# Hybrid decoder layer on one core: all decay blocks of an HGRN2 head in one TensorE visit, ordered by tile width

## The chip, the cores and the metric

The kernel runs on one core of a Trainium2 chip. The metric is the device time of one execution in microseconds (us); lower is better. TensorE (PE in the profile) does matrix products, VectorE (DVE) and ScalarE (ACT) do element-wise work, SyncE (SP) issues the loads from HBM.

## What is computed

One layer of a decoder for 256 tokens of width 2048, in float32: a token mixer with two branches (HGRN2, a gated linear attention with 16 heads of 128 channels, and Mamba-2 with 8 groups), then a cross attention into 256 memory tokens, then a gated convolutional feed-forward part and a last norm. The change lies in the HGRN2 branch, with a small part in Mamba-2. Cut to that:

```python
def gla_chunk_scan(q, k, v, log_f):
    ...
        b = jnp.cumsum(gc, axis=1)
        o_inter = jnp.einsum('bthk,bhkv->bthv', qc * jnp.exp(b), state)
        decay = masked_decay(b[:, :, None] - b[:, None, :])
        scores = jnp.einsum('bthk,btshk,bshk->bhts', qc, decay, kc)
        o_intra = jnp.einsum('bhts,bshv->bthv', scores, vc)
    ...
def hgrn2_branch(q_raw, f_raw, i_raw, og_raw, lb, norm_g):
    ...
    o = gla_chunk_scan(q, k, v, log_f)
    o = o * jax.nn.sigmoid(og_raw...)
    o = o * lax.rsqrt(jnp.mean(o * o, axis=-1, keepdims=True) + NORM_EPS)
    o = o * norm_g
```

The kernel does not walk through the tokens. For every head it makes the whole matrix A[s, t] of decayed scores (source token s, target token t, s not after t), and then weighs the values with it.

## The kernel before, in words

**The main stream.** Nearly all work is products of 256 tokens with large weight matrices. A weight piece of 1 MB comes by DMA into `raw`; ACT casts it (line 103) into a high part `hi`, and DVE makes the rest `lo` (line 104), half a piece at a time, both into rings of five halves. `project` (line 171 on) takes one piece and makes 16 pairs of products on TensorE: `hi` with 512 columns (lines 157, 159) and `lo` with 256 columns (lines 156, 160). `project_tok` (lines 189 to 191) takes four pieces and makes token rows with 512 columns each; it is called once for every four heads. Operands of these products are float32r; the small products described below are plain float32, which the profile shows as two passes per product (two instructions).

**Side work in steps.** The recurrences are generators in the list `background`. Every call of `weights()`, that is, every time the main stream takes the next piece, calls `step()`, and every generator in the list then runs on to its next `yield`, the oldest first. So the side work's products come into TensorE's queue between two pieces: such a group of small products is called a visit here. One head of HGRN2 takes three pieces (query, forget gate, output gate; lines 376 to 384), and every fourth head four more before them (values). Only when a head's three projections are issued does its generator `hg_scan` enter the list. Its steps fall on the next six pieces:

1. Step 0 (lines 390 to 429): the gates. ACT and DVE make log f and its running sum `bb`, then differences and their exponentials for the levels of half width 2, 4, 8, 16, 32 and 64 (tiles `e0`, `e1`; view `lev`) and for the two halves of 128 tokens (`ec`).
2. Step 1 (lines 431 to 438): DVE multiplies them with keys and queries.
3. Step 2 (lines 447 to 465): TensorE makes the blocks of the levels 1 to 16: products whose left operand has 32 columns, so that four of them fill the four column groups of the array (lines 449 and 455), into the PSUM tile `lp`. DVE merges them into `sm` with masks (lines 459 to 464).
4. Step 3 (lines 467 to 487): TensorE makes, for each half of the tokens, the two blocks of level 32 (left operand of 32 columns, line 471) and the block of level 64 (64 columns, line 474), then the block between the halves (128 columns, line 477), into a `misc` tile. DVE and ACT copy everything into A (tile `a`; lines 480 to 487).
5. Step 4 (lines 490 to 496): TensorE weighs the values with A (lines 490, 491), DVE multiplies with the output gate `so` (line 492), and the squares are split in two parts (`sqs`, lines 494 to 496).
6. Step 5 (lines 498 to 506): TensorE sums the squares (line 500), ACT makes the norm, DVE applies it and splits the result (lines 504, 506).

With three pieces per head, steps 3, 4 and 5 of a head fall on the same pieces as steps 0, 1 and 2 of the next, except behind every fourth head.

**The order on each engine** is set when the program is built. A planner goes through the instructions in program order, and may put an instruction that it takes to be ready ahead of one that it takes to be waiting. On the chip every engine works through its own queue in that order and waits on semaphores.

**Mamba-2** has the same form: `m2_scan` (line 568 on) is a generator whose third visit makes the squares' sum (line 624); one group takes six pieces.

The names that matter: `pm_` ("misc", two PSUM tiles), `pl` ("lev", two PSUM tiles), `so` (two buffers), `ab` (two tiles A).

Of the kernel before, what the change touches and what calls it, by code (L numbers as in the profile page):

```python
# [9 lines left out]
F32 = mybir.dt.float32  # L10
# [9 lines left out]
P = 128  # L20
T = 256
# [6 lines left out]
HEADS = 16  # L28
GROUPS = 8
# [13 lines left out]
SMALL = 5  # L43
B = 32
# [5 lines left out]
def hybrid_trunk(ctx, tc, xT, memT, par, cst, msk, w_ka, w_va, w_hg, w_hv, w_ghg, w_bhg, w_dt,  # L50
# [13 lines left out]

# [1 line left out]
    order = [w_ka[n] for n in range(KD)]  # L66
# [26 lines left out]
    def halves(w, c, d):  # L93
        """Both float32r parts of the columns c..d of a piece of weights."""
        raw, cols, parts = w
        half = (cols // 256) * 128
        a, b = (0, half) if c < half else (half, cols)
        if c == a:
            hi = wp.tile([P, 1024], F32R, name="hi", bufs=WB)
            lo = wp.tile([P, 1024], F32R, name="lo", bufs=WB)  # L100
            parts.append((a, b, hi, lo))
        _, _, hi, lo = parts[-1]
        S.copy(out=hi[:, c - a:d - a], in_=raw[:, c:d])  # L103
        V.tensor_tensor(out=lo[:, c - a:d - a], in0=raw[:, c:d],  # L104
                        in1=hi[:, c - a:d - a].bitcast(F32), op=ALU.subtract)
# [23 lines left out]
    def drain():  # L129
        while background:  # L130
            step()

    def prefetch(ahead):
        while state["issued"] < min(state["used"] + ahead, len(order)):
            issue()
# [15 lines left out]

# [1 line left out]
    def hl_pair(ps, wh, wl, hl, first, last):  # L153
        """ps[:, 0:T] + ps[:, T:2T] gathers w @ x, but for the product of both low parts."""
        if last:
            PE.matmul(ps[:, 0:T], lhsT=wl, rhs=hl[:, 0:T], start=False, stop=False)  # L156
            PE.matmul(ps, lhsT=wh, rhs=hl, start=first, stop=True)  # L157
        else:
            PE.matmul(ps, lhsT=wh, rhs=hl, start=first, stop=False)  # L159
            PE.matmul(ps[:, 0:T], lhsT=wl, rhs=hl[:, 0:T], start=False, stop=False)  # L160
# [17 lines left out]
    def project_tok(hl):  # L178
        """Token rows: [128 tokens, 512 channels] for both halves of the tokens."""
        ps = [pj.tile([P, 512], F32, name="proj") for _ in range(2)]  # L180
        for i in range(4):
            w = weights()
            for j in range(4):
                k = 4 * i + j
                wh, wl = w(j, 512)
                for g in range(2):
                    x1 = hl[:, k, g * P:(g + 1) * P]
                    x2 = hl[:, k, T + g * P:T + (g + 1) * P]
                    PE.matmul(ps[g], lhsT=x1, rhs=wh, start=(k == 0), stop=False)  # L189
                    PE.matmul(ps[g], lhsT=x1, rhs=wl, start=False, stop=False)  # L190
                    PE.matmul(ps[g], lhsT=x2, rhs=wh, start=False, stop=(k == KD - 1))  # L191
        return ps
# [33 lines left out]
    def row_rsqrt(pool, out, acc):  # L226
        """1/rms of every token, on all partitions."""
        ps = pm_.tile([P, 512], F32, name="misc")
        PE.matmul(ps[:, 0:T], lhsT=ones, rhs=acc, start=True, stop=True)
        rsqrt(out, ps[:, 0:T], 1.0 / D, eps_t)  # L230

    def col_rsqrt(out, acc):
        """1/rms of every token, tokens on partitions."""
        ps = pm_.tile([P, 512], F32, name="misc")
        for g in range(2):
            PE.matmul(ps[:, g:g + 1], lhsT=acc[:, g * P:(g + 1) * P], rhs=ones[:, 0:1],
                      start=True, stop=True)
        rsqrt(out, ps[:, 0:2], 1.0 / D, eps_t)

# [1 line left out]
    s1 = big.tile([P, KD, 512], F32R, name="s1")  # L241
# [25 lines left out]
    with tc.tile_pool(name="st", bufs=1) as st:  # L267
# [6 lines left out]
        r_xb = st.tile([P, T], F32, name="r_xb")  # L274
        # the first chunks advance together, so that the products need little data at a time
        nc.sync.dma_start(out=par_t[:, 0:8 * KD], in_=par[:, 0:8 * KD])
# [45 lines left out]

        # lower bounds and the per-channel constants made of them
        lb = st.tile([P, 4, KD], F32, name="lb")
# [26 lines left out]

# [1 line left out]
    def softplus_neg_abs(x, w, absolute=False):  # L353
        """w = ln(1 + exp(-|x|))"""
        if not absolute:
            S.activation(out=w, in_=x, func=AF.Abs)
            x = w
        S.activation(out=w, in_=x, func=AF.Exp, scale=-1.0)
        S.activation(out=w, in_=w, func=AF.Ln, bias=1.0)
# [27 lines left out]
    def hg_scan(h, kq, zz, v):  # L387
# [17 lines left out]
        S.activation(out=kq[:, 0, :], in_=t, func=AF.Exp, scale=-1.0)  # L405
        so = mp.tile([P, T], F32, name="so", bufs=2)
        V.scalar_tensor_tensor(out=so, in0=zz[:, 1, :], scalar=0.0, in1=w[:, 1, :],
                               op0=ALU.min, op1=ALU.subtract)
        S.activation(out=so, in_=so, func=AF.Exp)

        # decayed keys (left half of a block) and queries (right half), per level; in blocks of
        # two tokens the left factor is one and the right one is the token's own decay
        ql = mp.tile([P, T // B, B + B // 2], F32, name="ql", bufs=1)
# [26 lines left out]

        # A[s, t]: own block of the first half | second half seen from the first | own block.
        # Within blocks of 32 tokens the levels are merged on a compact [s, half, t of the block].
        a = ab[h % 2]
        lp = pl.tile([P, 512], F32, name="lev")
        W1 = B + B // 2
        for g in range(2):
            for blk in range(P // B):
# [3 lines left out]
            for i, hw in enumerate(LEVELS[1:SMALL]):  # L451
                o = 2 * W1 + (2 * i + g) * B
                for blk in range(P // B):
                    t0 = g * P + blk * B
                    PE.matmul(lp[blk * B:(blk + 1) * B, o:o + B], lhsT=lev[hw][:, t0:t0 + B],  # L455
                              rhs=lev[hw][:, t0:t0 + B], start=True, stop=True)
        sm = mp.tile([P, 2, B], F32, name="sm", bufs=1)
        l0 = lp[:, 0:2 * W1].rearrange("p (g t) -> p g t", g=2)
# [3 lines left out]
        for i in range(1, SMALL):  # L462
            o = 2 * W1 + 2 * (i - 1) * B
            V.copy_predicated(out=sm, mask=free(msk_t, i * B, [(0, 2), (1, B)]),
                              data=lp[:, o:o + 2 * B].rearrange("p (g t) -> p g t", g=2))
        yield True
        ps = pm_.tile([P, 512], F32, name="misc")
        for g in range(2):
            for s0 in (0, 2 * B):
                t0 = g * P + s0  # L470
                PE.matmul(ps[s0:s0 + B, g * B:(g + 1) * B], lhsT=lev[32][:, t0:t0 + B],  # L471
                          rhs=lev[32][:, t0 + B:t0 + 2 * B], start=True, stop=True)
            t0 = g * P
            PE.matmul(ps[0:2 * B, P + 2 * g * B:P + 2 * (g + 1) * B],  # L474
                      lhsT=lev[64][:, t0:t0 + 2 * B], rhs=lev[64][:, t0 + 2 * B:t0 + 4 * B],
                      start=True, stop=True)
        PE.matmul(ps[:, T:3 * P], lhsT=ec[:, 0:P], rhs=ec[:, P:T], start=True, stop=True)  # L477
        for blk in range(P // B):
            rows = slice(blk * B, (blk + 1) * B)
            V.tensor_copy(out=free(a[rows, :], blk * B, [(2 * P, 2), (1, B)]), in_=sm[rows])  # L480
        for s0 in (0, 2 * B):
            rows = slice(s0, s0 + B)
            V.tensor_copy(out=free(a[rows, :], s0 + B, [(2 * P, 2), (1, B)]),
                          in_=ps[rows, 0:2 * B].rearrange("p (g t) -> p g t", g=2))
        V.tensor_copy(out=free(a[0:2 * B, :], 2 * B, [(2 * P, 2), (1, 2 * B)]),
                      in_=ps[0:2 * B, P:T].rearrange("p (g t) -> p g t", g=2))
        S.copy(out=a[:, P:2 * P], in_=ps[:, T:3 * P])
        yield True
        ps = pm_.tile([P, 512], F32, name="misc")
# [6 lines left out]
        split(sqs, sq)  # L496
        yield True
        ps = pm_.tile([P, 512], F32, name="misc")
# [12 lines left out]

# [1 line left out]
    dt_tok = cp.tile([P, 2, 32], F32, name="dt_tok")  # L513
    cum_tok = cp.tile([P, 2, 32], F32, name="cum_tok")

    def m2_dt():
# [14 lines left out]
        V.memset(one[0:32], 1.0)  # L531
        cum = mp.tile([P, T], F32, name="so", bufs=2)
        V.tensor_tensor_scan(out=cum[0:32], data0=one[0:32], data1=w[0:32], initial=0.0,
# [34 lines left out]
    def m2_scan(g, sz, cb):  # L568
# [50 lines left out]
        V.tensor_tensor(out=sq[:, 0, :], in0=sq[:, 0, :], in1=sq[:, 1, :], op=ALU.add)  # L619
        yield True  # L620
        if g + 1 < GROUPS:
            yield True
        ps = pm_.tile([P, 512], F32, name="misc")
# [44 lines left out]

# [1 line left out]
    xp = ctx.enter_context(ExitStack())  # L670
# [104 lines left out]

# [1 line left out]
    fp = ctx.enter_context(tc.tile_pool(name="fp", bufs=1))  # L777
# [67 lines left out]

# [1 line left out]
def _cols(w):  # L847
    """[K, N] -> [N/128, 128 rows of a k block, K/128 * 128]"""
    k, n = w.shape
# [4 lines left out]
def _toks(w):  # L854
    """[K, N] -> [N/512, 4, 128 rows of a k block, 4 * 512]"""
    k, n = w.shape
# [91 lines left out]
```

## Time and profile before

| | |
|---|---|
| device time, three runs | 2317.78 us median (2317.59 to 2318.37) |
| the profiled execution: its span | 2318.0 us (0.2 us above the median of the runs) |
| granted TensorE clock, mean | 0.998 |
| HGRN2: from the first visit to the last | 155.2 to 542.1 us of the span |
| Mamba-2: from its first visit to its last | 728.7 to 1017.0 us of the span |

The profiled execution's own time is its span, 2318.0 us. A row of the timeline has the start in us, the duration in us, the engine, the line, the operation, output<-input tiles and the number of instructions merged. A TensorE instruction's duration includes the way through the array, so starts, not durations, tell what a product costs in a stream: the next one starts before the last one has ended.

### The profile page before, as it was taken

The page shows a single profiled execution, that of the slowest core. Times are in us where ns is not written, and L with a number is a line of the kernel's source. Part 1 is how long each engine was busy: PE and PEld are TensorE (multiplying, and loading weights), DVE is VectorE, ACT ScalarE, POOL GpSimd, SP SyncE. Part 2 cuts the span into 40 slices and gives each one's busy share as a digit, 9 for nine tenths or more (in the row PEclk, how much of TensorE's full clock was granted, in tenths as well). Part 3 has the DMA queues.
Part 4 walks back from the last instruction along what each step waited for, and adds up shares of the span by engine and source line. Part 5 has one row for each costly group of instructions (what it writes and reads, how often), then busy time and mean ns, then how long its engine had stood idle before and what let it go on. Part 6 is the DMA issues. An engine that isn't in the chain of part 4 may idle for free.

```text
span 2318.0 us, 35910 instructions
## 1 busy us (share of the span) xinstructions
PE 2298.1 (99%) x14210; PEld 1983.4 (86%) x14210; DVE 1610.9 (69%) x2652; ACT 1348.4 (58%) x2126; POOL 1.3 (0%) x9
## 2 busy tenths in 40 slices
PE   8999999999999999999999999999999999999998
PEld 7888888888888888888888888888888888888887
DVE  7768879797556777765676755667777777765554
ACT  7566767676445778764455645555555555544443
POOL 0000000000000000000000000000000000000000
PEclk9999999999999999999999999999999999999999
DMA  7654444445555455445566544555555555545554
GB/s 276 243 182 162 167 164 164 164 164 208 184 183 190 174 190 184 180 173 190 182 232 213 206 167 164 186 213 187 186 190 188 182 185 191 187 159 195 197 194 141
DMA packets 74953, 433.93 MB, mean 187 GB/s; under 512 B 8321, under 2 KB 15905, under 8 KB 31009
## 3 DMA queue, kind: packets, MB, share of 16 engines
q1 hardware_dynamic: 74208, 430.72, 52.7%
q8 instruction: 112, 1.84, 0.3%
q10 hardware_dynamic: 576, 0.92, 0.1%
q14 instruction: 57, 0.46, 0.1%
HBM read 425.28 MB, written 6.32 MB: 186 GB/s over the span
## 4 chain that ended last, share of the span: by engine, by line
PE 98%; DVE 1%; ACT 0%; DMA 0%; SPq 0%; issue 0%; DVEq 0%; ACTq 0%
PE proj L159 53%; PE proj L160 27%; PE proj L157 3%; PE proj L189 3%; PE proj L191 3%; PE proj L190 3%; PE proj L156 2%; PE misc L159 0%; DMA mraw<-in_memT 0%; PE lev L455 0%; PE misc L608 0%; PE misc L474 0%; PE misc L490 0%; PE misc L477 0%; PE misc L471 0%; PE misc L157 0%
## 5 line engine op out<-in xcount | busy, mean ns | idle before, releaser
L159 PE MATMUL proj<-s,hi 128*128 128x512 f32 x4935 | 1760.9, 399 | 9.9 <-ACT hi L103 5.5
L160 PE MATMUL proj<-s,lo 128*128 128x256 f32 x4935 | 1385.1, 281 | 0.0
L104 DVE TENSOR_TENSOR lo<-raw,hi 128x1024 fp32r<-128x1024 f32 (+4 forms) x827 | 956.8, 1161 | 410.3 <-ACT hi L103 402.4
L159 PEld LDWEIGHTS proj<-s,hi 128*128 128x128 f32 x4935 | 928.3, 188 | 223.6 <-ACT hi L103 11.3
L103 ACT CAST hi<-raw 128x1024 fp32r<-128x1024 f32 (+4 forms) x827 | 824.2, 998 | 431.2 <-PE proj L159 284.1
L160 PEld LDWEIGHTS proj<-s,lo 128*128 128x128 f32 x4935 | 933.1, 189 | 12.5 <-DVE lo L104 0.3
L196 ACT COPY jt<-proj 128x256 f32<-128x256 f32 x265 | 98.4, 372 | 384.2 <-PE proj L157 384.1
L157 PE MATMUL proj<-s,hi 128*128 128x512 f32 x313 | 124.9, 399 | 0.0
L159 PE MATMUL proj<-ha,hi 128*128 128x512 f32 x300 | 106.5, 398 | 0.0
L189 PE MATMUL proj<-hi,s 128*128 128x512 f32 x256 | 101.0, 395 | 0.0
L191 PE MATMUL proj<-hi,s 128*128 128x512 f32 x256 | 99.8, 390 | 0.0
L190 PE MATMUL proj<-lo,s 128*128 128x512 f32 x256 | 99.7, 389 | 0.0
L156 PE MATMUL proj<-s,lo 128*128 128x256 f32 x313 | 88.2, 282 | 0.0
L160 PE MATMUL proj<-ha,lo 128*128 128x256 f32 x300 | 84.2, 281 | 0.0
L156 PEld LDWEIGHTS proj<-s,lo 128*128 128x128 f32 x313 | 58.8, 188 | 15.2
L159 PEld LDWEIGHTS proj<-ha,hi 128*128 128x128 f32 x300 | 56.4, 188 | 13.3
L157 PEld LDWEIGHTS proj<-s,hi 128*128 128x128 f32 x313 | 59.3, 190 | 0.2 <-DVE s L212 0.2
L197 DVE TENSOR_TENSOR t<-proj,jt 128x256 f32<-128x256 f32 x65 | 27.5, 424 | 44.6 <-ACT jt L196 44.5
L160 PEld LDWEIGHTS proj<-ha,lo 128*128 128x128 f32 x300 | 56.7, 189 | 0.7
L191 PEld LDWEIGHTS proj<-hi,s 128*128 128x128 f32 x256 | 48.0, 188 | 10.2
L190 PEld LDWEIGHTS proj<-lo,s 128*128 128x128 f32 x256 | 48.1, 188 | 9.6
L189 PEld LDWEIGHTS proj<-hi,s 128*128 128x128 f32 x256 | 48.1, 188 | 9.4
(273 smaller groups left out, 1682.7 us busy)
## 6 DMA issues: line engine op xcount, KB each, us to landing
raw<-in_w_up SPq DMA_DIRECT2D x88, 1024.0 KB, 4.8
raw<-in_w_hg SPq DMA_DIRECT2D x48, 1024.0 KB, 4.8
raw<-in_w_m SPq DMA_DIRECT2D x48, 1024.0 KB, 4.8
raw<-in_w_dn SPq DMA_DIRECT2D x64, 704.0 KB, 4.1
raw<-in_w_hv SPq DMA_DIRECT2D x16, 1024.0 KB, 4.9
raw<-in_w_ghg SPq DMA_DIRECT2D x16, 1024.0 KB, 4.8
raw<-in_w_bhg SPq DMA_DIRECT2D x16, 1024.0 KB, 4.8
raw<-in_w_gm SPq DMA_DIRECT2D x16, 1024.0 KB, 4.8
```

What stands on the lines that cost most here:

```text
L103: S.copy(out=hi[:, c - a:d - a], in_=raw[:, c:d])
L104: V.tensor_tensor(out=lo[:, c - a:d - a], in0=raw[:, c:d], in1=hi[:, c - a:d - a].bitcast(F32), op=ALU.subtract)
L156: PE.matmul(ps[:, 0:T], lhsT=wl, rhs=hl[:, 0:T], start=False, stop=False)
L157: PE.matmul(ps, lhsT=wh, rhs=hl, start=first, stop=True)
L159: PE.matmul(ps, lhsT=wh, rhs=hl, start=first, stop=False)
L160: PE.matmul(ps[:, 0:T], lhsT=wl, rhs=hl[:, 0:T], start=False, stop=False)
L189: PE.matmul(ps[g], lhsT=x1, rhs=wh, start=(k == 0), stop=False)
L190: PE.matmul(ps[g], lhsT=x1, rhs=wl, start=False, stop=False)
L191: PE.matmul(ps[g], lhsT=x2, rhs=wh, start=False, stop=(k == KD - 1))
L196: S.copy(out=tmp, in_=ps[:, T:2 * T])
L197: V.tensor_tensor(out=out, in0=ps[:, 0:T], in1=tmp, op=ALU.add)
```

## The change

Step 3's products move into step 2, ahead of the narrow ones, so that one visit makes all blocks in the order 128, 64 and 32 columns. The block between the halves gets a second `lev` tile (`ep`), the blocks of the levels 64 and 32 go into the unused columns of `lp`, and the two level-64 blocks now lie in the two column halves of the array. The weighing and the norm come three steps later each, where the next head's blocks are made: in the same visit come, in this order, the norm of head h-2, the weighing of head h-1 and the blocks of head h. The copies into A follow at once. `so` has four buffers in place of two. In Mamba-2 the norm of a group comes three steps later, with the visit of the next group's first products.

```diff
+    def pause(n):
+        for _ in range(n):
+            yield True
...
-        so = mp.tile([P, T], F32, name="so", bufs=2)
+        so = mp.tile([P, T], F32, name="ho", bufs=4)
...
         lp = pl.tile([P, 512], F32, name="lev")
+        ep = pl.tile([P, 512], F32, name="lev")
         W1 = B + B // 2
+        o32 = 2 * W1 + 2 * (SMALL - 1) * B
+        o64 = o32 + 2 * B
+        PE.matmul(ep[:, 0:P], lhsT=ec[:, 0:P], rhs=ec[:, P:T], start=True, stop=True)
+        for g in range(2):
+            t0 = g * P
+            PE.matmul(lp[g * 2 * B:(g + 1) * 2 * B, o64:o64 + 2 * B],
+                      lhsT=lev[64][:, t0:t0 + 2 * B], rhs=lev[64][:, t0 + 2 * B:t0 + 4 * B],
+                      start=True, stop=True)
+        for g in range(2):
+            for s0 in (0, 2 * B):
+                t0 = g * P + s0
+                PE.matmul(lp[s0:s0 + B, o32 + g * B:o32 + (g + 1) * B], lhsT=lev[32][:, t0:t0 + B],
+                          rhs=lev[32][:, t0 + B:t0 + 2 * B], start=True, stop=True)
         for g in range(2):
             for blk in range(P // B):
...
+        S.copy(out=a[:, P:2 * P], in_=ep[:, 0:P])
         sm = mp.tile([P, 2, B], F32, name="sm", bufs=1)
...
-        yield True
-        ps = pm_.tile([P, 512], F32, name="misc")
+        for s0 in (0, 2 * B):
+            rows = slice(s0, s0 + B)
+            V.tensor_copy(out=free(a[rows, :], s0 + B, [(2 * P, 2), (1, B)]),
+                          in_=lp[rows, o32:o64].rearrange("p (g t) -> p g t", g=2))
         for g in range(2):
-            for s0 in (0, 2 * B):
-                t0 = g * P + s0
-                PE.matmul(ps[s0:s0 + B, g * B:(g + 1) * B], lhsT=lev[32][:, t0:t0 + B],
-                          rhs=lev[32][:, t0 + B:t0 + 2 * B], start=True, stop=True)
-            t0 = g * P
-            PE.matmul(ps[0:2 * B, P + 2 * g * B:P + 2 * (g + 1) * B],
-                      lhsT=lev[64][:, t0:t0 + 2 * B], rhs=lev[64][:, t0 + 2 * B:t0 + 4 * B],
-                      start=True, stop=True)
-        PE.matmul(ps[:, T:3 * P], lhsT=ec[:, 0:P], rhs=ec[:, P:T], start=True, stop=True)
+            V.tensor_copy(out=a[0:2 * B, 2 * g * P + 2 * B:2 * g * P + 4 * B],
+                          in_=lp[g * 2 * B:(g + 1) * 2 * B, o64:o64 + 2 * B])
...
-        yield True
+        gap = 3 if h + 1 < HEADS else 2
+        yield from pause(gap)
...
-        yield True
+        yield from pause(gap)
...
-        yield True
-        if g + 1 < GROUPS:
-            yield True
+        yield from pause(5 if g + 1 < GROUPS else 1)
```

More of the change, by code (lines that the diff above doesn't have):

```diff
@@ L480, in hg_scan @@
             V.tensor_copy(out=free(a[rows, :], blk * B, [(2 * P, 2), (1, B)]), in_=sm[rows])
[L481 to L487, printed above, removed]
-        yield True
+        gap = 3 if h + 1 < HEADS else 2
+        yield from pause(gap)
         ps = pm_.tile([P, 512], F32, name="misc")
@@ L531, in m2_dt @@
         V.memset(one[0:32], 1.0)
-        cum = mp.tile([P, T], F32, name="so", bufs=2)
+        cum = mp.tile([P, T], F32, name="ho", bufs=4)
         V.tensor_tensor_scan(out=cum[0:32], data0=one[0:32], data1=w[0:32], initial=0.0,
```

## The prediction

> **What bounds the kernel now.** First the page: engine totals and the chain that ended last.
>
> ```profile
> span 2318.0 us, 35910 instructions
> PE 2298.1 (99%) x14210; PEld 1983.4 (86%) x14210; DVE 1610.9 (69%) x2652; ACT 1348.4 (58%) x2126; POOL 1.3 (0%) x9
> PE 98%; DVE 1%; ACT 0%; DMA 0%; SPq 0%; issue 0%; DVEq 0%; ACTq 0%
> ```
>
> TensorE works through its queue almost without a wait. So what counts is how far each group of instructions moves TensorE's next start; the busy column can't tell, since durations overlap. I therefore took the timeline of TensorE alone, at head 7, whose visits look like those of any head. This is step 3 (levels 32 and 64, block between the halves):
>
> ```profile
> 303.59 0.40 PE L157 MATMUL proj<-s,hi 128*128 128x512 f32 x1
> 303.92 0.26 PE L471 MATMUL misc<-e 128*32 128x32 f32 x4
> 304.11 0.33 PE L474 MATMUL misc<-e 128*64 128x64 f32 x2
> 304.37 0.26 PE L471 MATMUL misc<-e 128*32 128x32 f32 x4
> 304.55 0.33 PE L474 MATMUL misc<-e 128*64 128x64 f32 x2
> 304.81 0.49 PE L477 MATMUL misc<-ec 128*128 128x128 f32 x2
> 305.06 0.47 PE L189 MATMUL proj<-hi,s 128*128 128x512 f32 x1
> 305.37 0.39 PE L190 MATMUL proj<-lo,s 128*128 128x512 f32 x1
> 305.60 0.40 PE L191 MATMUL proj<-hi,s 128*128 128x512 f32 x1
> ```
>
> A product of 512 columns moves the next start by 0.23 us (305.37 to 305.60). So the stream could have gone on at 303.82; it goes on at 305.06, and its first product takes 0.31. The visit costs 1.24 + 0.08 = 1.32 us, for twelve small products. The tile width (128*32, 128*64, 128*128) changes five times; the entry alone, 303.82 to 303.92, is 0.10 us with nothing in it. Step 4 (weighing) and steps 5 and 2 (norm, then narrow blocks):
>
> ```profile
> 310.62 0.59 PE L490 MATMUL misc<-a,vc 128*128 128x256 f32 x2
> 311.06 0.38 PE L491 MATMUL misc<-a,vc 128*128 128x128 f32 x2
> 311.19 0.47 PE L189 MATMUL proj<-hi,s 128*128 128x512 f32 x1
> 311.51 0.39 PE L190 MATMUL proj<-lo,s 128*128 128x512 f32 x1
> ...
> 316.74 0.40 PE L500 MATMUL misc<-sqs,ones_r 128*128 128x256 f32 x2
> 317.07 0.29 PE L449 MATMUL lev<-ql,kq 128*32 128x48 f32 x8
> ...
> 317.94 0.50 PE L189 MATMUL proj<-hi,s 128*128 128x512 f32 x1
> 318.28 0.40 PE L190 MATMUL proj<-lo,s 128*128 128x512 f32 x1
> ```
>
> The weighing costs 0.57 + (0.32 - 0.23) = 0.66 us, the other visit 1.20 + (0.34 - 0.23) = 1.31. One head's side work costs 1.32 + 0.66 + 1.31 = 3.29 us of TensorE's stream, 16 heads some 53 us.
>
> DVE is the second bound. One head's period within a run of heads, in the view by stretches (stretch, length, then busy time of PE, PEld, DVE, ACT):
>
> ```profile
> 277.20:297.20 20.00, 20.00 (x197) 17.21 (x196) 18.66 (x47) 15.15 (x29) 0.00 (x0) 1.00 0.46 159
> ```
>
> 18.66 of 20.00 us: little room, and the products of step 2 need what DVE makes last.
>
> **The change part by part.**
>
> *TensorE's visits.* The joint visit has norm, weighing, block between the halves (all 128 wide), two level-64 blocks, four level-32 blocks, narrow blocks.
> - Norm: half of a 512-column product for each of two, 0.23. Weighing: 0.66, as now.
> - Block between the halves: the weighing streams 384 columns in two passes for 0.66, so 128 columns cost 0.22. Its own row is dearer (304.81 to 305.06, 0.25, and the 0.08 behind it), since it now stands behind a width change. I take 0.22; upper end 0.33.
> - Entry into the narrow widths: 0.10, as at 303.82.
> - Level 64: one block with its way out takes 0.26 (304.11 to 304.37). The two blocks now lie in two column halves. What that does, Mamba-2 shows (L584 full width, L608 in two halves):
>
> ```profile
> 728.69 0.59 PE L584 MATMUL misc<-sz 128*128 128x256 f32 x2
> 729.12 0.38 PE L585 MATMUL misc<-sz 128*128 128x128 f32 x2
> 735.43 0.66 PE L608 MATMUL misc<-e,bb 128*64 128x256 f32 x4
> 735.91 0.40 PE L610 MATMUL misc<-e,bb 128*64 128x128 f32 x4
> ```
>
>   Two passes take 0.43, four in two halves 0.48: they run side by side. So I take 0.28 for both blocks, upper end 0.52.
> - Level 32: four passes with the way out 0.19 (303.92 to 304.11), of which I take 0.12 as the way out to the next width (an estimate: the entry's 0.10 and the last pass). Eight passes with no width change behind them: 0.13; upper end 0.25.
> - Narrow blocks: 317.07 to 317.94 and 0.11 behind, 0.98.
>
> Sum 0.23 + 0.66 + 0.22 + 0.10 + 0.28 + 0.13 + 0.98 = 2.60 us against 3.29: 0.69 saved per head, 11.0 us for 16. With all upper ends it is 3.07, 0.22 saved, 3.5 us. Heads behind the value projections have the blocks alone in their visit, at the same saving, since norm and weighing cost nothing beyond their columns wherever they stand. So the shared visit itself saves nothing; the saving is in the fewer width changes, three in place of seven.
>
> The Trainium skill (TensorEngine Tiling (Array Packing), Key Properties) says that a change of tiling mode, not of tile, drains TensorE. By it alone, at the entry's 0.10 for each of four changes, the saving would be 0.40 a head, 6.4 us; the rows give more, because a way back to the stream costs another 0.08 to 0.11 at its first product, and the level-64 blocks pair up.
>
> *New wait: the wide blocks come first, and are made from DVE's last results.* Head 5:
>
> ```profile
> 264.02 0.37 ACT L196 COPY jt<-proj 128x256 f32<-128x256 f32 x1 [1.89 <-PE proj L157]
> 266.20 0.27 ACT L487 COPY a<-misc 128x128 f32<-128x128 f32 x1 [0.33 <-DVE a L485]
> 265.83 0.28 DVE L485 COPY a<-misc 64x128 f32<-64x128 f32 x1
> 268.12 0.43 DVE L396 TENSOR_TENSOR lf<-lf,w 128x256 f32<-128x256 f32 x1 [0.75 <-ACT w L359]
> 276.47 0.43 DVE L438 TENSOR_TENSOR ec<-ec,kq 128x256 f32<-128x256 f32 x1
> 277.20 0.29 PE L449 MATMUL lev<-ql,kq 128*32 128x48 f32 x8
> ```
>
> The head's last projection is read at 264.02, its chain (gates, sum, differences, multiplies) ends at 276.90, and its blocks start at 277.20, 13.18 after the reading. Between the two lie the visits of steps 3 and 4 of the head before, 1.32 + 0.66. They go; the weighing now stands ahead of the blocks in their own visit, so the blocks come at 13.18 - 1.32 = 11.86. The chain takes 12.88. It gets shorter too: without step 3's copies between 264 and 266.4 ACT need not wait 0.33 and copy 0.27, and can go on some 0.6 earlier; the weighing's two DVE operations (L492 and the split of `sqs`) leave the chain's second part, 0.35 each by the next fence's six in 2.10. That is 1.3, so the chain ends at about 11.6, 0.26 ahead of need. Behind the joint visit DVE has more in one heap: all copies, one more of them (two of 64x64 for L485's 0.28), and the operations of weighing and norm. They are queued ahead of the next head's chain on DVE, and the period is 0.7 shorter with DVE at 18.7 of 19.3. I price the wait at 0 to 0.4 us, 0.1 on average, for 12 heads: 1.2 us. Queued behind the waiting product is the whole stream.
>
> For the first head behind the value projections there are no visits on the way now either:
>
> ```profile
> 237.61 0.48 DVE L504 SCALAR_TENSOR_TENSOR so<-so,par_t,r 128x256 f32<-128x256 f32 x1
> 255.46 0.42 DVE L438 TENSOR_TENSOR ec<-ec,kq 128x256 f32<-128x256 f32 x1
> 255.79 2.10 DVE L435 TENSOR_TENSOR e<-e,kq 128x256 f32<-128x256 f32 x6
> 257.20 0.29 PE L449 MATMUL lev<-ql,kq 128*32 128x48 f32 x8
> ```
>
> The blocks start at 257.20; level 64 is multiplied last, until 257.89. Today nobody waits for it. In the new order it is wanted 0.32 behind the start (0.22 + 0.10): 0.4 us of waiting. For heads 4, 8 and 12 the norm of the head before also falls into this chain (L504 0.48 and a split of 0.35, which today come from 237.61 on): up to 1.2. I take 0.8 for these three, 0.4 for head 0: 2.8 us. Bounds 0 (the planner puts level 64 earlier) and 5.
>
> *The rest.* Mamba-2's norm rides with the next group's products:
>
> ```profile
> 748.24 0.59 PE L624 MATMUL misc<-bb,ones 128*128 128x256 f32 x2
> 748.49 0.58 PE L159 MATMUL proj<-s,hi 128*128 128x512 f32 x1
> 748.90 0.28 PE L160 MATMUL proj<-s,lo 128*128 128x256 f32 x1
> ...
> 1024.69 0.50 PE L159 MATMUL proj<-s,hi 128*128 128x512 f32 x1 [0.45 <-DVE s L212]
> ```
>
> 0.25 + (0.41 - 0.23) = 0.43 is just its two passes (728.69 to 729.12), full width before and after: nothing is saved. At the end of the groups TensorE waits 0.45 for the last group's result, and the norm before it moves closer: 0 to 1 us, I take 0.3. More buffers for `so`, a second `lev` tile and one `misc` tile less free nobody and hold nobody, as TensorE waits for no tile now. No DMA moves.
>
> Sum: -11.0 + 1.2 + 2.8 + 0.3 = -6.7 us.
>
> **The rivals.**
> 1. *Nothing waits.* The planner, which sorts by its own idea of readiness, has level 64 and `ec` done in time. For: in head 5 `ec` is multiplied behind the levels, at the first head ahead of them, so it does move them. Against: DVE at 18.66 of 20.00. Saving 10.7: 2307.1.
> 2. *The wait eats the saving.* The chain is late by 0.5 in twelve heads and by 1.2 in four: 6.0 + 4.8 against 11.0. No change: 2317.6. Against: the 1.3 us that leave the chain.
> 3. *Slower.* One mechanism: DVE's queue behind the joint visit. Masks, copies, weighing and norm and the `lo` parts that DVE put off do not fit between the visit and the next reading of a projection, and the chain's first DVE operation (L396) starts late, by 1.0 us in twelve heads and with 1.2 in four: 12.0 + 4.8 - 11.0 = +5.8, 2323.6. It decides from 0.5 us per head on. For: L396 stands behind them in a strict queue; against: DVE waits 0.75 for ACT there, so some of the delay costs nothing.
> 4. *The change doesn't do what it says*: the planner tears the blocks apart, so that part of them goes into the stream later. Each tear costs an entry, a way out and the stream's slower first product, 0.10 + 0.12 + 0.11 = 0.33; with one in every head 5.3 of 11.0 are gone and no wait is left: 2312.1. That is near my forecast, by another way.
>
> **How the numbers follow.** Against the median of 2317.78: 2317.8 - 6.7 = 2311.1 us. Chances: the forecast with rival 4, 0.54; rival 1, 0.18; rival 2, 0.17; rival 3, 0.11. What a measurement can tell from no change is 0.2%, 4.6 us: below 2313.2 is faster. So faster 0.72, same 0.17, slower 0.11. The range goes from 2305.5 (rival 1 with level 32 and 64 at their cheapest) to 2319.5, which holds rival 2 and leaves out rival 3 and some of each edge. The likeliest case's own range is 2307 to 2314.
>
> **What would show it.** Right: one visit per head with widths 128, 64, 32 in this order, 2.6 us from its first product to the stream's, no second entry; level-64 passes in pairs; weighing 0.66 unchanged. A wait on TensorE's weight loads ahead of the first wide block, put down to DVE's multiplies (L438, L435), longest at heads 4, 8 and 12. DVE over 95% in a head's period. Wrong: level-64 blocks one behind the other (visit of 2.9), a wait of over 0.5 us in the ordinary heads, or a gap in the main stream put down to `lo` or `hi`.

## The result and the profile after

The changed kernel takes 2326.78 us, median of five runs (2325.33 to 2327.32), against 2318.37 for the kernel before in the same session. The ratio is 1.0035, 95% interval [1.0024, 1.0046]: slower by about a third of a per cent, where 6.7 us less were forecast. The profiled execution has a span of 2325.5 us, 1.3 below its median, at a granted clock of 0.998 as before. First the page of the changed kernel: engine totals, and the chain that ended last.

```profile
PE 2295.8 (99%) x14210; PEld 1980.4 (85%) x14210; DVE 1611.9 (69%) x2668; ACT 1344.7 (58%) x2122; POOL 1.3 (0%) x9
PE 89%; DVE 6%; ACT 4%; issue 1%; DMA 0%; SPq 0%; DVEq 0%; ACTq 0%
```

TensorE's busy time went down by 2.3 us while the span grew by 7.5, and its share of the chain fell from 98 to 89%. Waits have come in. TensorE's waits in the changed kernel that the kernel before doesn't have (waiting line <- line waited for: us in total, times, longest):

```profile
PE misc L618 <- DVE e L602: 6.5, 10, 0.7
PE lev L455 <- ACT r L220: 2.2, 3, 1.0
PE lev L455 <- DVE ec L442: 2.0, 6, 0.5
PE lev L458 <- DVE e L439: 1.2, 5, 0.3
```

The largest is L618 (L608 before), a product of Mamba-2; the other three are HGRN2's blocks, 5.4 us of waiting that the view puts down to ACT's and DVE's results. Of Mamba-2 the prediction expected no wait in the groups.

To place the difference I use one mark that all kernels share: the last product of a projection (L157 before, L161 after). The starts of its 20th, 76th and 151st row are 149.18, 581.47 and 1029.09 us before, and 147.66, 579.08 and 1036.66 after. From the first to the second mark lies HGRN2's stage, from the second to the third Mamba-2's. The start-up ahead of the first mark, which no kernel changes, varies by up to 3 us from profile to profile, so spans alone would mislead. HGRN2 goes from 432.29 to 431.41 us (0.9 less, where 7.0 less were forecast), Mamba-2 from 447.62 to 457.59 (10.0 more, where 0.3 were). All experiments, in this measure:

| kernel | us, beside before in the same session | ratio [95%] | HGRN2 | Mamba-2 |
|---|---|---|---|---|
| after | 2326.78, 2318.37 | 1.0035 [1.0024, 1.0046] | -0.87 | +9.97 |
| e2: before, Mamba-2's part alone | 2327.9, 2318.57 | 1.0040 [1.0026, 1.0055] | +0.94 | +9.77 |
| e1: after, without Mamba-2's part | 2316.48, 2318.57 | 0.9992 [0.9983, 1.0001] | -0.87 | +0.04 |
| e3: after, Mamba-2's norm one piece earlier | 2317.92, 2318.57 | 0.9998 [0.9988, 1.0007] | -0.86 | +1.80 |
| e4: after, norm issued behind the products | 2317.08, 2317.59 | 0.9999 [0.9988, 1.0011] | -0.95 | +1.39 |
| e13: after, norm applied one piece later | 2318.89, 2317.37 | 1.0005 [0.9995, 1.0016] | -1.29 | +2.52 |
| e5: e1, blocks one piece later | 2309.06, 2318.57 | 0.9959 [0.9944, 0.9974] | -8.13 | +0.04 |
| e6: e1, narrow blocks first | 2318.04, 2317.59 | 1.0002 [0.9991, 1.0013] | +0.46 | 0.00 |
| e7: e5, widths alternating | 2316.23, 2317.59 | 0.9994 [0.9983, 1.0005] | -0.91 | +0.05 |
| e8: e5, no shared visit | 2316.05, 2317.59 | 0.9993 [0.9982, 1.0005] | -1.12 | +0.05 |
| e9: e1, without copies into A | 2311.05, 2317.22 | 0.9971 [0.9960, 0.9983] | -5.89 | +0.05 |
| e11: e1, four copies on GpSimd | 2311.8, 2317.22 | 0.9978 [0.9967, 0.9989] | -5.55 | 0.00 |
| e12: e5 with e11 | 2307.9, 2317.37 | 0.9959 [0.9945, 0.9973] | -8.95 | 0.00 |

Seven of these intervals hold 1; for them the two stages, taken from one profile each, carry the reading. An unchanged Mamba-2 repeats within about 0.05 us. HGRN2's stage is less steady: e2 leaves its code alone, every engine works through it in the same order as before, and it takes 0.94 us more. So a difference of under 1 us in that column is not an effect that these profiles show, and the 0.87 us of the changed kernel is one of them, though e1, e3 and e4 repeat it.

e10, the same kernel as e13, ran ahead of it; its profiled execution took 3192.23 us at a granted clock of 0.65, so it has no row here, and its other one took 2318.94.

**Mamba-2, one group.** The joint visit, with the norm of the group before, passes without a wait. The next visit, with the products of line 618, does not. TensorE's timeline there in the changed kernel (start, duration, engine, line, operation, tiles, count, and in brackets the idle time before it):

```profile
939.60 0.39 PE L161 MATMUL proj<-s,hi 128*128 128x512 f32 x1
940.73 0.66 PE L618 MATMUL misc<-e,bb 128*64 128x256 f32 x4 [0.74 <-DVE e L602]
...
942.18 0.66 PE L618 MATMUL misc<-e,bb 128*64 128x256 f32 x4 [0.57 <-DVE e L602]
...
942.99 0.50 PE L163 MATMUL proj<-s,hi 128*128 128x512 f32 x1
```

and the same place before:

```profile
972.54 0.40 PE L157 MATMUL proj<-s,hi 128*128 128x512 f32 x1
...
974.37 0.50 PE L159 MATMUL proj<-s,hi 128*128 128x512 f32 x1
```

From the last product ahead of the visit to the first behind it are 3.39 us in place of 1.83. The two waits, 0.74 and 0.57, sit ahead of the two pairs of products. In five groups this visit costs 3.25 in place of 1.70, counted as in the prediction. All of Mamba-2's visits together cost 33.57 us in place of 25.89: 7.7 of the 10.0.

Why L602 is late, on DVE's timeline after:

```profile
938.44 0.48 DVE L636 SCALAR_TENSOR_TENSOR kq<-kq,par_t,r 128x256 f32<-128x256 f32 x1 [1.55 <-ACT r L220]
...
939.24 0.48 DVE L636 SCALAR_TENSOR_TENSOR kq<-kq,par_t,r 128x256 f32<-128x256 f32 x1
939.63 0.95 DVE L602 TENSOR_TENSOR e<-e,a 128x768 f32<-128x768 f32 x1
...
941.17 0.95 DVE L602 TENSOR_TENSOR e<-e,a 128x768 f32<-128x768 f32 x1
```

and on ACT's:

```profile
934.75 1.28 ACT L219 ACT_TABLE_LOAD   x1
936.05 0.47 ACT L219 ACTIVATE r<-misc,eps_t 128x256 f32<-128x256 f32 x1
936.42 0.26 ACT L600 COPY a<-misc 128x128 f32<-128x128 f32 x1
936.69 1.28 ACT L220 ACT_TABLE_LOAD   x1
937.99 0.42 ACT L220 ACTIVATE r<-r 128x256 f32<-128x256 f32 x1
```

The norm needs a logarithm and an exponential, with a table load of 1.28 ahead of each. L602 multiplies `e` with the copy of line 600, which is done at 936.68. It starts at 939.63, because L636, the norm of the group before, was put ahead of it in DVE's queue and waits until 938.44 for the exponential. So DVE stands still for 1.55 us with ready work behind it. The Trainium skill (TensorE: Matmul & The Clock Gate, the table at its top) says that ACT's, DVE's and GpSimd's queues are strictly first in, first out; for DVE this trace agrees, with 2.95 us between ready and start. Before, the same multiply started 0.28 us behind its copy:

```profile
968.11 0.25 ACT L590 COPY a<-misc 128x128 f32<-128x128 f32 x1
968.64 0.95 DVE L592 TENSOR_TENSOR e<-e,a 128x768 f32<-128x768 f32 x1
```

The view of DVE's waits shows why before's trace gave no warning. This is its row for the norm in Mamba-2's stage before:

```profile
DVE kq L628 <- ACT r L216: 16.7, 8, 2.4
```

and after:

```profile
DVE kq L636 <- ACT r L220: 11.6, 8, 2.3
```

DVE waited longer for the norm before. It cost nothing: none of TensorE's products in Mamba-2's visits waited then. What stands behind the waiting norm decides, as e13 shows below.

**HGRN2, head 6.** Heads are counted from 0 here, as in the prediction's heads 4, 5, 8 and 12; the visit that it calls head 7's, at 303.59, is head 6's by this count. TensorE after:

```profile
293.79 0.40 PE L510 MATMUL misc<-sqs,ones_r 128*128 128x256 f32 x2
...
294.60 0.48 PE L163 MATMUL proj<-s,hi 128*128 128x512 f32 x1
...
296.38 0.46 PE L455 MATMUL lev<-ec 128*128 128x128 f32 x2 [0.25 <-DVE ec L442]
296.77 0.34 PE L458 MATMUL lev<-e 128*64 128x64 f32 x4
297.04 0.28 PE L464 MATMUL lev<-e 128*32 128x32 f32 x5
```

There is no shared visit for this head. The planner went back to the main stream behind the weighing, as rival 4 had it, put the blocks into the middle of the next piece, and even there they wait for `ec`. The order of widths 128, 64, 32 is as written. The first head of every group has the block between the halves alone, ahead of the rest, and the other heads from 3 to 14 are torn like head 6. Only heads 1 and 2 have the visit that the change describes, head 2 with norm, weighing and blocks:

```profile
191.82 0.40 PE L510 MATMUL misc<-sqs,ones_r 128*128 128x256 f32 x2
...
192.71 0.39 PE L455 MATMUL lev<-ec 128*128 128x128 f32 x2
...
194.33 0.50 PE L163 MATMUL proj<-s,hi 128*128 128x512 f32 x1
```

It waits for nothing and costs 2.61 us by the prediction's count, where 2.60 was forecast.

### The profile page after: what moved, and what is told of

The parts are those of the page before. It is cut to its first block, busy times and chain, and to the rows that moved or that the text cites. A ratio compares the mean times of both kernels' runs of the same rounds, so it can differ in the third digit from the quotient of the medians.

```text
span 2325.5 us, 35932 instructions
## 1 busy us (share of the span) xinstructions
PE 2295.8 (99%) x14210; PEld 1980.4 (85%) x14210; DVE 1611.9 (69%) x2668; ACT 1344.7 (58%) x2122; POOL 1.3 (0%) x9
## 4 chain that ended last, share of the span: by engine, by line
PE 89%; DVE 6%; ACT 4%; issue 1%; DMA 0%; SPq 0%; DVEq 0%; ACTq 0%
PE proj L163 49%; PE proj L164 25%; PE proj L161 3%; PE proj L195 2%; PE proj L194 2%; PE proj L193 2%; ACT hi L103 2%; PE proj L160 1%; DVE lo L104 1%; DVE e L426 1%; DVE e L439 1%; PE misc L163 0%; ACT w L362 0%; DVE e L602 0%; PE lev L475 0%
## 5 line engine op out<-in xcount | busy, mean ns | idle before, releaser
L161 PE MATMUL proj<-s,hi 128*128 128x512 f32 x313 | 125.0, 399 | 0.0
L161 PEld LDWEIGHTS proj<-s,hi 128*128 128x128 f32 x313 | 59.4, 190 | 0.2 <-DVE s L216 0.2
```

## The experiments

**e2 and e1: Mamba-2's part alone, and everything but it.** e2 is the kernel before with one edit:

```diff
-        yield True
-        if g + 1 < GROUPS:
+        for _ in range(5 if g + 1 < GROUPS else 1):
             yield True
```

> The kernel before with Mamba-2's late norm alone. Theory M: 9 to 10 us slower than before, 2327.5 us; the products that follow wait 1.5 us in each of five groups. Rival (HGRN2's change is needed for the loss): 2318.

e1 is the changed kernel with

```diff
-        yield from pause(5 if g + 1 < GROUPS else 1)
+        yield from pause(2 if g + 1 < GROUPS else 1)
```

> The changed kernel with Mamba-2's norm back at its old place. Theory M (all of the loss lies in Mamba-2, where the norm of group g-1 now comes in one piece with the products of group g): the stretch of the Mamba-2 groups, which grew by 10.3 us, is as before; the whole is 1.3 us below the kernel before, 2317 us, and HGRN2 alone has nearly no gain. Rival (the loss comes out of HGRN2, whose delayed work runs on into Mamba-2): it stays at about 2326.

Measured: +9.77 us in Mamba-2's stage for e2, +0.04 for e1. The loss lies in those lines alone, whatever HGRN2 does. e2 also shows +0.94 in HGRN2, which it doesn't touch; I have no explanation for that. e1 leaves HGRN2's 0.9 us as they stand, and its time can't be told from before.

**e3, e4, e13: what in the late norm costs it.** The rivals are the order in DVE's queue, the table loads on ACT, and lateness as such. e3 pauses 4 in place of 5, so that the norm falls on a piece without the products.

> The changed kernel with Mamba-2's norm two pieces later than before in place of three, so in the piece ahead of the next group's products and not in one with them. Theory Q (what costs is that the norm's ScalarE and VectorE work stands in the same piece ahead of what the next products wait for): the loss goes, 2317 us, as with the norm at its old place. Rival (what costs is that the norm is late, or that it shares ScalarE's tables with the next group): still 5 us or more above that, 2322 to 2326.

e4 keeps norm and products in the same piece, with the norm issued behind the products (its squares get a tile of their own):

```diff
+        while late:
+            list(late.pop())
         yield True
         yp = pm_.tile([P, 512], F32, name="misc")
...
+        if g + 1 < GROUPS:
+            late.append(norm(g, y, sq))
```

> The changed kernel with Mamba-2's norm in the same piece as the next group's products, as in the change, but issued behind them and behind what ScalarE and VectorE make of them (the squares get a buffer of their own). Theory Q (order within the queues: the norm's logarithm and exponential with their table loads and its VectorE operations stand ahead of the operations that the next group's products wait for): the wait of those products goes, 2317 to 2318.5 us. Rival (the amount of work in the one piece is too much, in any order): still 2323 to 2327.

e13 leaves the logarithm and the exponential where the change has them, and puts off what follows them: DVE's multiplies, and the split of their result on ACT and DVE. The norm's tile `r` moves to another buffer for that:

```diff
-        r = mp.tile([P, T], F32, name="r", bufs=1)
+        r = mp.tile([P, T], F32, name="lf", bufs=1)
         rsqrt(r, ps[:, 0:T], 1.0 / T, eps2_t)
+        if g + 1 < GROUPS:
+            yield True
```

> The kernel with the norm's products, logarithm and exponential in the shared piece and VectorE's part one piece later, once more, for its stages. Theory V (VectorE's queue): Mamba-2 stage 0 to 2.5 us above before in place of 10.0, and the products that followed 1.5 us late stand where they stood before. Rival S (ScalarE's queue with its table loads): 6 to 10 us above.

In all three the visit of line 618 costs 1.69 to 1.70 us again in these groups, and Mamba-2's visits sum to 25.8 to 25.9, as before. e13 decides: ACT loads its tables at the same place, the copy of line 600 comes 3.76 us behind the joint visit's start in both kernels (932.09 and 936.42), up to there only DVE's queue is different, and the wait is gone. DVE's first multiply in e13:

```profile
932.47 0.96 DVE L602 TENSOR_TENSOR e<-e,a 128x768 f32<-128x768 f32 x1
```

The joint visit that makes its input starts at 928.33 in e13 and at 932.66 after: it starts 4.1 us behind it in place of 7.0. What stays, 1.4 to 2.5 us in the stage, is in no visit: between the visits the main stream takes that much longer, in the changed kernel too, where it is the 2.3 us beyond the 7.7. I have not found why. The same kernel as e13 had run earlier, as e10:

> The changed kernel; Mamba-2's late norm stays in one piece with the next group's products, and ScalarE's logarithm and exponential with their table loads too, but VectorE applies the norm one piece later. Theory V (VectorE's queue: the norm's first operation waits for ScalarE's exponential, and the multiply that the next products need stands behind it): the wait of those products goes, Mamba-2 stage 0 to 2.5 us above before in place of 10.0, 2316 to 2319. Rival S (ScalarE's queue: the table loads stand ahead of the copy that this multiply needs): 6 to 10 us above, 2323 to 2327.

Its 2318.94 us agree with theory V and with e13's 2318.89; it gives no stages.

**e5: the wide blocks with time to spare.** e1 with one more pause ahead of the blocks (besides, the tile `kq` of keys and queries is taken behind the head's first projection and not ahead of it; e7, e8 and e12 keep both):

```diff
         V.tensor_tensor(out=ecv, in0=ecv, in1=free(kq, 0, [(T + P, 2), (1, P)]), op=ALU.mult)
         yield True
+        yield True
         a = ab[h % 2]
```

> The changed kernel with Mamba-2's norm at its old place and every head's blocks one piece later (one more yield ahead of them; the tile of keys and queries is taken after the first projection). Theory W (the order by width saves 0.7 us a head, and TensorE's waits for VectorE's last multiplies eat nearly all of it): no wait is left in the visits, 16 times 0.68 saved, 2307.5 us. Rival (the order by width saves nothing, and there are no waits that matter): 2317, as the kernel with the norm back.

Head 6's visit in e5:

```profile
295.24 0.40 PE L506 MATMUL misc<-sqs,ones_r 128*128 128x256 f32 x2
295.48 0.59 PE L496 MATMUL misc<-a,vc 128*128 128x256 f32 x2
295.91 0.38 PE L497 MATMUL misc<-a,vc 128*128 128x128 f32 x2
296.13 0.39 PE L451 MATMUL lev<-ec 128*128 128x128 f32 x2
296.44 0.34 PE L454 MATMUL lev<-e 128*64 128x64 f32 x4
296.71 0.28 PE L460 MATMUL lev<-e 128*32 128x32 f32 x5
...
297.71 0.50 PE L193 MATMUL proj<-hi,s 128*128 128x512 f32 x1
298.05 0.40 PE L194 MATMUL proj<-lo,s 128*128 128x512 f32 x1
```

This is the visit that the change describes: one piece, no wait. By the prediction's own way of counting it costs 2.57 us, where 2.60 was forecast. The four level-64 passes take 0.27 (296.44 to 296.71; forecast 0.28), the block between the halves 0.31 with the entry into the next width (forecast 0.22 + 0.10). The visits of four heads (4 to 7) cost 12.94 us before, 12.63 in e1 and 10.29 in e5: 0.66 saved per head, and all but 0.08 of it lost again in e1. Over the whole stage the visits add up to 53.1 us before, 50.6 in e1 and 43.0 in e5, 0.7 of it a wait at the transposes of Mamba-2's time steps. The stage gains less than the visits do, 0.9 in place of 2.5 in e1 and 8.1 in place of 10.1 in e5: between the visits the main stream takes 1.6 and 2.0 us longer, which I have not traced (in e2 it takes 1.1 longer, with HGRN2's code unchanged).

**e6 and e7: the order of widths.** e6 is e1 with the narrow blocks first, then levels 32 and 64 and the block between the halves, so that the last results are needed last:

```diff
-        PE.matmul(ep[:, 0:P], lhsT=ec[:, 0:P], rhs=ec[:, P:T], start=True, stop=True)
...
         for g in range(2):
             for blk in range(P // B):
...
...
+        PE.matmul(ep[:, 0:P], lhsT=ec[:, 0:P], rhs=ec[:, P:T], start=True, stop=True)
```

> The changed kernel with Mamba-2's norm at its old place and a head's blocks in the reverse order, narrow ones first and the block between the halves last, in the same visit. Theory W (waits for VectorE's last multiplies, which the wide blocks need, eat the saving): the products that are ready first now cover part of the wait, some 0.3 us less per visit, 2311 to 2314. Rival (the whole of the multiplies is late, whatever is needed first): 2316 to 2317, as with the wide ones first.

e7 is e5 with the level-32 and level-64 blocks alternating, half by half, as step 3 had them:

```diff
         for g in range(2):
-            t0 = g * P
-            PE.matmul(lp[g * 2 * B:...], lhsT=lev[64]..., rhs=lev[64]...)
-        for g in range(2):
             for s0 in (0, 2 * B):
...
+            t0 = g * P
+            PE.matmul(lp[g * 2 * B:...], lhsT=lev[64]..., rhs=lev[64]...)
```

> The kernel with the blocks one piece later, with the levels 32 and 64 alternating by half of the tokens as before the change (three more width changes in each of 16 visits, and the two level-64 blocks no longer side by side). Theory W (order by width saves): 0.5 us more per head by the rows of the kernel before (0.19 + 0.26 + 0.19 + 0.26 in place of about 0.41), 8 us, 2317. Rival (what the kernel with later blocks gains comes from fewer visits or easier queues, not from the order): 2309, as without.

e6 is 1.3 us worse than e1 in the stage. With the narrow blocks first, heads 5 to 7 cost a little less (2.93, 2.83 and 3.19 us for all that is in their visits, in place of 3.04, 3.06 and 3.40), but heads 4, 8 and 12 have their blocks torn into three parts and cost 2.74 in place of 2.04. So part of the wait can be covered by the order, and it brings nothing as a whole. e7 gives 7.2 of e5's 8.1 us back, 0.50 per head:

```profile
299.26 0.26 PE L455 MATMUL lev<-e 128*32 128x32 f32 x4
299.45 0.33 PE L458 MATMUL lev<-e 128*64 128x64 f32 x2
299.71 0.26 PE L455 MATMUL lev<-e 128*32 128x32 f32 x4
299.89 0.33 PE L458 MATMUL lev<-e 128*64 128x64 f32 x2
300.15 0.29 PE L464 MATMUL lev<-ql,kq 128*32 128x48 f32 x8
```

From 299.26 to 300.15 are 0.89 us. The level-64 blocks take 0.26 each, one behind the other, where e5's pair takes 0.27. So the order by width is worth what the prediction said, and its price is measured by itself.

**e8: does sharing the visit matter?** e5 with weighing and norm each in the next piece:

```diff
-        gap = 3 if h + 1 < HEADS else 2
+        gap = 1
```

> The kernel with the blocks one piece later, with weighing and norm one piece each behind the blocks, so that a head has three visits of its own again and no visit is shared. Theory W (products of full width cost their columns and nothing more, wherever they stand): 2309 us within 1.5 us. Rival (every visit has a price of its own, 0.1 to 0.3 us): 32 more visits, 3 to 10 us more, 2312 to 2319.

The block visit costs 1.68 and the weighing alone 0.65: TensorE pays nothing for visits of their own. Yet 7.0 of the 8.1 us are gone. The norm now has one piece to be ready in. Its two products read the two parts of the squares, of which ACT makes one until 293.52 and DVE the other until 294.01; the stream behind them goes on 0.71 us behind the first, where 0.23 would do:

```profile
293.11 0.41 ACT L215 CAST sqs<-sq 128x256 fp32r<-128x256 f32 x1
293.59 0.42 DVE L216 TENSOR_TENSOR sqs<-sq,sqs 128x256 fp32r<-128x256 f32 x1
293.57 0.88 PE L506 MATMUL misc<-sqs,ones_r 128*128 128x256 f32 x2
294.28 0.39 PE L163 MATMUL proj<-s,hi 128*128 128x512 f32 x1
```

The norm costs 0.80 to 1.11 us in place of 0.23 in eleven heads, some 7 us. What the change's spacing brings is time for ACT and DVE between the steps.

**e9 and e11: why the blocks are late in the changed kernel.** The theory: DVE's heap of copies behind a visit stands ahead of the next head's gates. e9 is e1 with the eight DVE copies into A left out, so that A holds only the block between the halves; e11 moves four of them to GpSimd:

```diff
-            V.tensor_copy(out=free(a[rows, :], blk * B, [(2 * P, 2), (1, B)]), in_=sm[rows])
+            G.tensor_copy(out=free(a[rows, :], blk * B, [(2 * P, 2), (1, B)]), in_=sm[rows])
```

> The changed kernel with Mamba-2's norm at its old place, and without VectorE's eight copies of a head's blocks into A (A keeps the block between the halves only; the rest of its weighing is left out). By stages of the trace, the kernel with the norm back stands 0.9 us below before in the HGRN2 stage. Theory D (VectorE's heap behind a visit, of which the copies are some 1.5 us, stands ahead of the next head's gates, so that the chain to the next blocks ends late): the chain's first sum (L400 there) comes about 1 us earlier after the projection, the waits in the visits go down by half or more, HGRN2 stage 4 to 7 us below before, 2310 to 2313. Rival P (the path to the blocks has become too short because two visits left it; VectorE's queue has no part): HGRN2 stage within 1.5 us of the kernel with the norm back, 2316.

> The changed kernel with Mamba-2's norm at its old place and the four copies of the merged narrow blocks into A on GpSimd, which has nothing else to do here. Theory D: 0.75 us less in VectorE's heap, the chain ends some 0.5 us earlier, HGRN2 stage 2 to 5 us below before, 2312 to 2315. Rival P: as with the norm back, 0.9 us below, 2316. If GpSimd's copies slow VectorE down at their common memory port, above before.

DVE after, behind head 5's visit, up to head 6's `ec`:

```profile
283.25 0.77 DVE L496 COPY a<-sm 32x64 f32<-32x64 f32 x4
284.05 0.42 DVE L201 TENSOR_TENSOR sz<-proj,jt 128x256 f32<-128x256 f32 x1
...
288.14 0.42 DVE L400 TENSOR_TENSOR lf<-lf,w 128x256 f32<-128x256 f32 x1
...
295.82 0.42 DVE L442 TENSOR_TENSOR ec<-ec,kq 128x256 f32<-128x256 f32 x1
```

with ACT's two steps around it:

```profile
282.69 0.37 ACT L200 COPY jt<-proj 128x256 f32<-128x256 f32 x1 [1.84 <-PE proj L161]
284.51 0.63 ACT L394 ACTIVATE w<-sz 128x512 f32<-128x512 f32 x1 [0.50 <-DVE sz L201]
```

and DVE in e9:

```profile
280.66 0.42 DVE L201 TENSOR_TENSOR sz<-proj,jt 128x256 f32<-128x256 f32 x1 [0.90 <-ACT jt L200]
285.18 0.42 DVE L400 TENSOR_TENSOR lf<-lf,w 128x256 f32<-128x256 f32 x1
289.71 0.42 DVE L442 TENSOR_TENSOR ec<-ec,kq 128x256 f32<-128x256 f32 x1
```

After, the projection is read at 282.69, the copies run until 284.02, the chain's first DVE step is at 284.05, ACT waits 0.50 for it, and L400 comes 5.45 us behind the reading (4.1 before: 264.02 to 268.12). `ec` is done 13.55 behind the reading. In e9, where the reading is at 280.26, L400 comes at 4.92 and `ec` is done at 9.87, ahead of the levels and not behind them: with DVE less full the planner also multiplies in another order. HGRN2 gains 5.9 us in e9 and 5.6 in e11, where nothing is left out and half of the copies only change engine. So the copies' place on DVE makes most of the wait. By which way is not settled: the gates come only 0.5 us earlier in e9 (4.92 against 5.45), and `ec` 3.7, most of it by the other order. In the changed kernel itself heads 1 and 2 have their copies ahead of them too, but the order of e9: their `ec` is done 10.09 us behind the reading, and they lose only 0.26 and 0.04 us to e5.

**e12: the best of these.** e5 with e11's copies.

> The kernel with the blocks one piece later, and the four copies of the merged narrow blocks on GpSimd. Theory D with W: no visit waits any more, so a lighter VectorE buys nothing more on TensorE, 2308 to 2310, as without GpSimd. Rival (VectorE still holds up the stream somewhere in HGRN2): 2305 to 2307.

2307.9 us, ratio 0.9959 [0.9945, 0.9973]. It beats before and after, but not e5 by anything the runs can tell: once the blocks have their piece, the copies are no longer in the way.

## Why the prediction was wrong

**The step that failed is "The rest".** It says of Mamba-2's norm: "0 to 1 us, I take 0.3". It is 10.0 us, of which 7.7 are waits in the visits of five groups. The columns were counted rightly: the joint visit costs 1.52 us, the group's first products alone cost 1.09, so the norm is 0.43 as forecast. But the step looked only at TensorE and at the end of the groups. The norm's other instructions, ACT's two functions with two table loads and DVE's two operations waiting for them, were moved too, to just ahead of the DVE work that TensorE needs next. No rival had it, so the range could not hold it. Shown by e1, e2, and, as to the cause of the 7.7 us, by e13; the other 2.3 stay open.

**"New wait" failed second.** It prices the ordinary heads at 0.1 us. By their visits in e1 against e5 they lose 0.68, 0.48 and 0.82 us in heads 5 to 7, and 0.60 on average over the eleven ordinary heads ahead of the last (from 0.04 in head 2 to 1.22 in head 3); six of them are over the 0.5 that the prediction names as a sign of being wrong. The step took 1.3 us out of the chain and priced the copies' heap at 0.1; the chain got longer instead, 13.55 in place of the forecast 11.6 in head 6. First heads of a group lose 0.36 (head 0 0.26), as a tear, in place of 0.8 and 0.4. Together that is 7.9 us in fifteen heads, where 4.0 were forecast for all sixteen, of the 10.6 that the order saves; the last head's visits hold Mamba-2's products too and can't be compared. With rival 2's price, and past the 0.5 us per head at which rival 3 decides, HGRN2 ended near no change, and not slower.

**Rival 4** was right in that the planner tears the visit in most heads, wrong in that then no wait is left: the blocks wait part of a piece later too.

**"TensorE's visits" was right**: 0.69 forecast per head, 0.66 measured in e5. "So the shared visit itself saves nothing" holds for TensorE's columns and fails as a sentence about the kernel: by e8 the spacing that comes with it is worth 7.0 us, through ACT and DVE.

## What to carry to other kernels

A step that is moved takes its instructions on every engine along; for each, ask what stands behind it in that engine's queue at the new place, and who needs that next. A wait on a side engine that costs nothing today is no evidence that it costs nothing elsewhere. To order small products by tile width is worth its price only when the last made operands have the time: e5's one more pause turned 0.9 us into 8.1 in the stage.

## What the runs showed that I had not expected

Two table loads of 1.28 us each come with every norm of Mamba-2, and the next function starts 0.02 us behind the load (936.03 to 936.05). The Trainium skill (ScalarE: Activation LUTs, What ACT_TABLE_LOAD costs) puts a drain of about 1380 ns to the load's 1283; the load agrees, the drain isn't to be seen in these rows.

e11's GpSimd copies run beside DVE with no loss that the stages show (5.6 us gained against 5.9 with the copies gone).
